# Two of the four sums of each block of w_out made by accumulating transfers in three of four column groups of a hybrid encoder layer

## The chip, the cores and the metric

The kernel runs on one core of a Trainium2 chip. The metric is the device time of one launch in microseconds, the median of several runs. The reader needs the names of the engines as the profile has them: PE multiplies matrices (PEld is its loading of weights), DVE and ACT work elementwise, POOL is a third elementwise engine that can also issue transfers, and SP issues nearly all transfers between HBM and the core's memory.

## The reference

One layer of an encoder on 512 tokens of width 2048, in float32. The input is normalised and multiplied by `w_in`. One part of the result goes through attention of 8 heads, another through a gated linear recurrence; both are normalised and gated. What matters here is the last step: the two halves are put side by side (512 x 2048) and multiplied by `w_out` (2048 x 2048), and the input is added:

```
mixed = jnp.concatenate([rms_norm(attn_out, attn_norm_w) * jax.nn.silu(g_attn),
                         rms_norm(lru_out, lru_norm_w) * jax.nn.silu(g_lru)], axis=-1)
return x + jnp.einsum('bse,ed->bsd', mixed, w_out)
```

## The kernel before

Every float32 product is made of three products of rounded parts: a matrix is cast to a high part on ACT (`wh`, `mh`), the rest is the low part, made by a subtraction on DVE (`wl`, `ml`), and PE multiplies high by high, high by low and low by high.

The last stage is `outputs` (L699 on). It works through `w_out` in four column groups of 512 columns (`c`), and in each group through eight blocks of 256 rows (`i`, 0 to 7 below). Six blocks (0 to 5) are multiplied by a scheme of Strassen's kind (Winograd's form): the block of 256 x 512 is cut into four quarters of 128 x 256, and seven products (`P1`, `Q6`, `Q5`, `Q7`, `P2`, `Q3`, `Q4`, L655) stand in place of eight. `mult` (L714) issues them, 42 matmuls of 256 columns for a block; `P1` needs only quarters of the block itself, `Q6` comes second and needs a sum. Blocks 6 and 7 are multiplied as they are (`whole`, L732). The left side has been split and summed beforehand.

What a block of the first kind needs before PE can take it, in `seven` (L674):

- `wraw` (L186) loads the block, 512 KB, from SP into a tile `wr`, of which there are three (L192).
- `combine` (L660) makes four sums of quarters into `t4`, a tile of 128 x 4 x 256 (the profile calls it `t`), of which there are two. The first two quarters, `src[:, 0]` and `src[:, 1]`, are the upper half of the block (its first 128 rows), left and right; the change calls them b12 and b11. `src[:, 2]` and `src[:, 3]` are the lower half, left and right. L665 makes the first two sums with one instruction, b11 + b12 and lower left + b12; L666 adds the lower left quarter to the first of them, and L667 adds the lower right one to the result.
- ACT casts three quarters of the block and then the four sums to the high parts (both L679), and DVE subtracts for the low parts (both L680). The tiles for these, `wkept` (L690), exist three times over: a block can be cast once PE is done with the block three before it.

For blocks 6 and 7 `four` (L682) casts and subtracts the quarters alone (L684, L685). After block 5 the products are put together on ACT (L775) and DVE (L776 to L779) and added to the input tile `xt` (L782); after block 7 DVE adds the remaining sums (L788, four adds for the four blocks of tokens) and SP stores each result (L789). The input for the next group is loaded by L708. In the first group, the left sides of the last blocks are still being made (`next(work)`, L758).

The order on PE is written out by hand. On the other engines a scheduler sets it: the blocks' preparation is given a high priority (`tc.high_priority(AHEAD)`), and each engine, SP and POOL among them, takes its instructions in the order in which the scheduler has put them; one that waits holds up those behind it. A tile that is used again can be written once its last reader is done.

Of the kernel before, what the change touches and what calls it, by code (L numbers as in the profile page):

```python
# [13 lines left out]
ALU = mybir.AluOpType  # L14
AX = mybir.AxisListType

P = 128
SEQ = 512
# [27 lines left out]
H = 256  # L46
# [9 lines left out]
def hybrid_kernel(  # L56
# [20 lines left out]
    nc = tc.nc  # L77
# [28 lines left out]
    def nm(s):  # L106
        cnt[0] += 1
        return f"{s}_{cnt[0]}"
# [30 lines left out]
    def f(ap):  # L139
        return ap.bitcast(F32)  # L140
# [45 lines left out]
    def wraw(w, r0, c0, nk=1):  # L186

        raw = pools["wr"].tile([P, 2, SEQ], F32, tag="wr", bufs=3, name=nm("wr"))
        src = w[r0 : r0 + 2 * P, c0 : c0 + SEQ].rearrange("(k p) e -> p k e", p=P)
        for k in range(nk):  # L190
            ks = slice(k * 2 // nk, (k + 1) * 2 // nk)
            nc.sync.dma_start(raw[:, ks, :], src[:, ks, :])  # L192
            yield raw
# [434 lines left out]
    def fin_s(shape=(P, SEQ)):  # L628
        return pools["fin"].tile(list(shape), F32, tag="s", bufs=2, name=nm("s"))
# [27 lines left out]
    def halves(t):  # L657
        return t.rearrange("p k (j e) -> p (k j) e", e=H)

    def combine(src, op):  # L660

        res = pools["fin"].tile([P, 4, H], F32, tag="t4", bufs=2, name=nm("t4"))
        a = nc.vector.tensor_tensor
        if op == ALU.add:
            a(res[:, 0:2], src[:, 1:3], src[:, 0:1].broadcast_to([P, 2, H]), op=op)  # L665
            a(res[:, 2], res[:, 0], src[:, 2], op=op)  # L666
            a(res[:, 3], res[:, 2], src[:, 3], op=op)  # L667
        else:
            a(res[:, 0:2], src[:, 0:1].broadcast_to([P, 2, H]), src[:, 1:3], op=op)
            a(res[:, 2], src[:, 1], res[:, 1], op=op)  # L670
            a(res[:, 3], src[:, 3], res[:, 2], op=op)
        return res

    def seven(src, op, hi, lo):  # L674

        src = halves(src)
        res = combine(src, op)
        for to, part in ((slice(0, 3), src[:, 1:4]), (slice(3, 7), res)):
            nc.scalar.copy(hi[:, to], part)  # L679
            nc.vector.tensor_sub(lo[:, to], part, f(hi[:, to]))  # L680

    def four(src, hi, lo):  # L682
        src = halves(src)
        nc.scalar.copy(hi, src)  # L684
        nc.vector.tensor_sub(lo, src, f(hi))  # L685
# [4 lines left out]
    def wkept(n):  # L690
        i = turn_of[0] % 3
        turn_of[0] += 1
        pool = pools["out" if i else "fin"]
        return [
            pool.tile([P, 7, H], F32R, tag=f"{t}{i}", bufs=1, name=nm(t))[:, :n]
            for t in ("wh", "wl")
        ]

    def outputs(work):  # L699

        for c in range(DM // SEQ):
# [12 lines left out]
            def mult(k, s, ah, al, a, bh, bl, b_, last):  # L714
                ts_ = slice(s * P, (s + 1) * P)
                if k in acc:
                    dst, bank = acc[k][:, s, :], k
                else:
                    bank = s if k == Q4 else 2 + s
                    dst = own[bank][:, H:] if k in (P2, Q4) else own[bank][:, :H]  # L720
                for lh, rh in ((ah, bh), (ah, bl), (al, bh)):
                    nc.tensor.matmul(  # L722
                        dst, lh[:, a, ts_], rh[:, b_, :], start=bank in fresh,
                        stop=last and s == 1 and rh is bh and lh is al, skip_group_check=True,
                    )
                    fresh.discard(bank)
# [5 lines left out]
            def whole(t, ah, al, bh, bl, last):  # L732

                ts_ = slice(t % 2 * P, (t % 2 + 1) * P)
                for half in range(2 if t == 1 and end else 1):
                    for k in range(2):
                        a, w = 2 * k + t // 2, slice(2 * k, 2 * k + 2)
                        dst = own[t].rearrange("p (j e) -> p j e", e=H)
                        if t == 1 and end:
                            dst, w = lasts[half], 2 * k + half  # L740
                        for j, (lh, rh) in enumerate(((ah, bh), (ah, bl), (al, bh))):
                            new = t == 1 and end and half == 0 and k == 0 and j == 0 and not last
                            nc.tensor.matmul(  # L743
                                dst, lh[:, a, ts_], rh[:, w], start=new,
                                stop=last and k == 1 and j == 2, skip_group_check=True,
                            )

            for i, (r0, A) in enumerate(mixed):
                with tc.high_priority(AHEAD):
                    (raw,) = wraw(w_out, r0, c * SEQ)  # L750
                    if i < 6:
                        bh, bl = wkept(7)
                        seven(raw, ALU.add, bh, bl)
                    else:
                        bh, bl = wkept(4)
                        four(raw, bh, bl)
                if c == 0:
                    next(work, None)  # L758
                    A = mixed[i][1]
                ah, al = A  # L760
                if i < 6:
                    for k in (P1, Q6, Q5, Q7, P2, Q3, Q4):
                        for s in range(2):
                            mult(k, s, ah, al, k[0], bh, bl, k[1], i == 5 and k in (P1, Q6, Q5, Q7))
                else:
                    for t in (2, 3, 0, 1):
                        whole(t, ah, al, bh, bl, i == 7)
                if i == 5:
                    with tc.high_priority(AHEAD):

                        def blk(i, j):
                            return comb[:, 2 * i : 2 * i + 2, j * H : (j + 1) * H]

                        v2 = fin_s((P, 2, H))
                        nc.scalar.copy(blk(1, 1), acc[P1])  # L775
                        nc.vector.tensor_sub(v2, acc[Q6], blk(1, 1))  # L776
                        nc.vector.tensor_add(blk(1, 0), acc[Q5], v2)
                        nc.vector.tensor_add(blk(0, 0), acc[Q7], blk(1, 0))
                        nc.vector.scalar_tensor_tensor(  # L779
                            blk(0, 1), acc[Q7], -1.0, v2, op0=ALU.mult, op1=ALU.subtract  # L780
                        )
                        nc.vector.tensor_add(xt, xt, comb)  # L782
# [124 lines left out]
    def build(i, pair, where, n=7):  # L907
        mixed[i][1] = hi, lo = where(n)
        if n == 7:
            seven(pair, ALU.subtract, hi, lo)  # L910
        else:
            four(pair, hi, lo)
# [28 lines left out]
    def last_gates():  # L941
# [11 lines left out]
        yield  # L953

    outputs(last_gates())
    closed("out", "wr", "cp")
    closed("fin", "hq")
# [41 lines left out]
```

## Time and profile before

| | |
|---|---|
| Median of three runs | 668.37 us (668.06 to 668.39) |
| The profiled execution's own time | 668.27 us |
| Its span in the profile | 666.5 us |
| DVE, ACT, POOL busy | 486.1, 331.1, 56.8 us |
| Bytes read from and written to HBM | 66.25 MB, 4.19 MB |
| PE's granted clock in the span | 1.00 |

The span runs from the first to the last instruction on the core; the execution's own time has the launch around it as well. A row of instructions by line gives the engine, the line, the operation, what it writes from what (`t<-wr`), how many there are, and the least, middle and longest duration of one in ns. A row of the timeline gives start and duration in us. A row of the transfers gives how many, their size, and the middle time from issue to landing in us. "SPq" is the queue of transfers that SP issues.

### The profile page before, as it was taken

What the parts mean: (1) busy time and instruction counts of PE and PEld (TensorE: products, weight loads), DVE (VectorE), ACT (ScalarE), POOL (GpSimd) and SP (SyncE); (2) the same over time, 40 slices, a digit from 0 to 9 for tenths busy, and PEclk for the clock granted to TensorE, in tenths of its full rate; (3) what the DMA queues carried; (4) which work ended last, traced back from release to release, by engine and by line L of the source; (5) the groups of instructions that cost most, each with busy time, mean ns of one, the idle gap of its engine ahead of it and who ended that gap; (6) DMA issues with size and microseconds to landing.
All of it is one profiled execution on the core that took longest, in us unless ns stands there. A gap on an engine that the chain in (4) does not pass through costs nothing.

```text
span 666.5 us, 9524 instructions
## 1 busy us (share of the span) xinstructions
PE 660.7 (99%) x3610; PEld 569.6 (85%) x3610; DVE 486.1 (73%) x819; ACT 331.1 (50%) x581; POOL 56.8 (9%) x77
## 2 busy tenths in 40 slices
PE   8999999999999999999999999999999999999997
PEld 6888888888888888888888888888889999899996
DVE  4879688978687754756955577449979994976944
ACT  4533898589766416345743455335436333332320
POOL 0000000000022203011222212110000000000000
PEclk9999999999999999999999999999999999999999
DMA  8842252323234412322112221232336364362711
GB/s 286 281 138 89 65 166 63 95 63 96 68 122 127 117 41 58 100 64 63 35 62 64 63 61 35 67 92 69 101 115 190 96 211 137 122 208 82 248 38 63
DMA packets 43773, 71.06 MB, mean 107 GB/s; under 512 B 2776, under 2 KB 13136, under 8 KB 43728
## 3 DMA queue, kind: packets, MB, share of 16 engines
q1 hardware_dynamic: 43696, 70.45, 34.5%
q8 instruction: 28, 0.46, 0.3%
q14 instruction: 17, 0.14, 0.1%
q10 hardware_dynamic: 32, 0.01, 0.0%
HBM read 66.25 MB, written 4.19 MB: 106 GB/s over the span
## 4 chain that ended last, share of the span: by engine, by line
PE 98%; DMA 1%; SPq 0%; DVE 0%; issue 0%
PE pj L143 20%; PE pj L145 20%; PE pj L144 20%; PE pj L722 10%; PE mm L722 8%; PE mm L743 6%; PE mm L145 3%; PE mm L143 3%; PE mm L144 3%; PE mm L568 2%; DMA b<-in_x_dram 1%; PE mm L229 1%; PE mm L516 1%; PE mm L266 0%; PE mm L636 0%; PE pj L743 0%
## 5 line engine op out<-in xcount | busy, mean ns | idle before, releaser
L143 PE MATMUL pj<-x,wh 128*128 128x512 f32 x384 | 153.1, 399 | 0.0
L145 PE MATMUL pj<-x,wl 128*128 128x512 f32 x384 | 149.9, 390 | 0.0
L144 PE MATMUL pj<-x,wh 128*128 128x512 f32 x384 | 149.7, 390 | 0.0
L203 ACT CAST wh<-wr 128x512 fp32r<-128x512 f32 x144 | 86.5, 617 | 81.2 <-PE pj L145 28.3
L204 DVE TENSOR_TENSOR wl<-wr,wh 128x512 fp32r<-128x512 f32 x144 | 100.6, 720 | 34.7 <-ACT wh L203 34.7
L145 PEld LDWEIGHTS pj<-x,wl 128*128 128x128 f32 x384 | 72.1, 188 | 15.4
L144 PEld LDWEIGHTS pj<-x,wh 128*128 128x128 f32 x384 | 72.3, 188 | 14.0 <-issue 0.5
L143 PEld LDWEIGHTS pj<-x,wh 128*128 128x128 f32 x384 | 72.2, 188 | 14.0 <-issue 0.5
L143 PE MATMUL pj<-wh,x 128*128 128x512 f32 x192 | 75.9, 395 | 0.0
L144 PE MATMUL pj<-wl,x 128*128 128x512 f32 x192 | 75.1, 391 | 0.0
L145 PE MATMUL pj<-wh,x 128*128 128x512 f32 x192 | 75.0, 391 | 0.0
L722 PE MATMUL pj<-wh,ml 128*128 128x256 f32 x192 | 54.1, 282 | 0.0
L722 PE MATMUL pj<-wh,mh 128*128 128x256 f32 x192 | 54.0, 281 | 0.0
L722 PE MATMUL pj<-wl,mh 128*128 128x256 f32 x192 | 53.8, 280 | 0.0
L679 ACT CAST wh<-wr 128x768 fp32r<-128x768 f32 x24 | 20.1, 836 | 60.9 <-issue 46.2
L570 ACT CAST b<-mm 128x512 fp32r<-128x512 f32 x32 | 18.8, 586 | 60.0 <-PE mm L568 60.0
L556 DVE TENSOR_REDUCE mx<-mm 128x1 f32<-128x512 f32 x32 | 22.1, 689 | 31.3 <-PE mm L145 30.8
L145 PEld LDWEIGHTS pj<-wh,x 128*128 128x128 f32 x192 | 36.1, 188 | 8.1
L143 PEld LDWEIGHTS pj<-wh,x 128*128 128x128 f32 x192 | 36.1, 188 | 8.0 <-issue 0.2
L144 PEld LDWEIGHTS pj<-wl,x 128*128 128x128 f32 x192 | 36.1, 188 | 7.9 <-issue 0.2
L722 PE MATMUL mm<-wh,ml 128*128 128x256 f32 x144 | 40.5, 282 | 0.0
L722 PE MATMUL mm<-wh,mh 128*128 128x256 f32 x144 | 40.5, 281 | 0.0
(203 smaller groups left out, 1322.3 us busy)
## 6 DMA issues: line engine op xcount, KB each, us to landing
wr<-in_w_in_dram SPq DMA_DIRECT2D x71, 512.0 KB, 3.6
wr<-in_w_out_dram SPq DMA_DIRECT2D x32, 512.0 KB, 3.8
xt<-in_x_dram SPq DMA_DIRECT2D x16, 256.0 KB, 4.4
out_dram<-xt SPq DMA_DIRECT2D x15, 256.0 KB, 3.6
b<-in_x_dram SPq DMA_DIRECT2D x7, 512.0 KB, 8.6
k<-in_lru_wa_dram SPq DMA_DIRECT2D x8, 128.0 KB, 3.7
k<-in_lru_wx_dram SPq DMA_DIRECT2D x8, 128.0 KB, 3.4
b<-in_x_dram SPq DMA_DIRECT2D x2, 256.0 KB, 4.9
```

The source lines that it names most:

```text
L143: nc.tensor.matmul(acc, lh, rh, start=start, stop=False)
L144: nc.tensor.matmul(acc, lh, rl, start=False, stop=False)
L145: nc.tensor.matmul(acc, ll, rh, start=False, stop=stop)
L203: nc.scalar.copy(hi, raw[:, k, :])
L204: nc.vector.tensor_sub(lo, raw[:, k, :], f(hi))
L229: nc.tensor.transpose(pt[:, t * P : (t + 1) * P], xc[:, t, ks], ident)
L556: nc.vector.tensor_reduce(mx, sc, axis=AX.X, op=ALU.max, negate=True)
L568: nc.tensor.transpose(pt[:, s * P : (s + 1) * P], p[:, s * P : (s + 1) * P], ident)
L570: nc.scalar.copy(pth[:, :, tt], p3)
L679: nc.scalar.copy(hi[:, to], part)
L722: nc.tensor.matmul(dst, lh[:, a, ts_], rh[:, b_, :], start=bank in fresh, stop=last and s == 1 and rh is bh and lh is al, skip_group_check ...
L743: nc.tensor.matmul(dst, lh[:, a, ts_], rh[:, w], start=new, stop=last and k == 1 and j == 2, skip_group_check=True,)
```

## The change

In `combine`, for the six blocks of the first kind in the column groups c = 1, 2 and 3 (`at` is None in the first group), the first instruction on DVE (L665) is replaced by three transfers. SP loads b11 into the first quarter of `t4` and the lower left quarter into the second, each 128 KB straight from `w_out` in HBM. POOL then issues one accumulating transfer, which adds b12 to both: it reads b12 from HBM twice (a source of step 0 over two) and adds it to what stands in `t4`. The first two quarters then hold the same two sums as before. The block itself is still loaded as before, and L666, L667 and all that follows stay as they are.

By the dependencies, the loads wait until `t4`'s buffer is free, the accumulating transfer waits for both loads, and L666 waits for the accumulating transfer.

```
-    def combine(src, op):
+    def combine(src, op, at=None):
 
         res = pools["fin"].tile([P, 4, H], F32, tag="t4", bufs=2, name=nm("t4"))
         a = nc.vector.tensor_tensor
         if op == ALU.add:
-            a(res[:, 0:2], src[:, 1:3], src[:, 0:1].broadcast_to([P, 2, H]), op=op)
+            if at:
+                r0, c0 = at
+                b12, b11 = (w_out[r0 : r0 + P, c0 + k * H : c0 + (k + 1) * H] for k in range(2))
+                nc.sync.dma_start(res[:, 0], b11)
+                nc.sync.dma_start(res[:, 1], w_out[r0 + P : r0 + 2 * P, c0 : c0 + H])
+                both = b12[:, None, :].broadcast_to([P, 2, H])
+                nc.gpsimd.dma_start(res[:, 0:2], both, accum_op=op)
+            else:
+                a(res[:, 0:2], src[:, 1:3], src[:, 0:1].broadcast_to([P, 2, H]), op=op)
             a(res[:, 2], res[:, 0], src[:, 2], op=op)
             a(res[:, 3], res[:, 2], src[:, 3], op=op)
...
-    def seven(src, op, hi, lo):
+    def seven(src, op, hi, lo, at=None):
 
         src = halves(src)
-        res = combine(src, op)
+        res = combine(src, op, at)
...
-                        seven(raw, ALU.add, bh, bl)
+                        seven(raw, ALU.add, bh, bl, (r0, c * SEQ) if c else None)
```

## Prediction

> **What bounds the kernel now.** I read the page's busy line first, then the waits of PE, then the chain of work that ended last.
>
> ```profile
> PE 660.7 (99%) x3610; PEld 569.6 (85%) x3610; DVE 486.1 (73%) x819; ACT 331.1 (50%) x581; POOL 56.8 (9%) x77
> PE mm L802 <- POOL ones L151: 1.1, 1, 1.1
> PE mm L229 <- DMA b<-in_x_dram: 0.9, 1, 0.9
> 540.15 2.80 PE pj L722 x24
> 581.12 2.80 PE pj L722 x24
> 621.72 2.88 PE pj L722 x24
> 646.64 2.88 PE pj L722 x24
> ```
>
> The second and third rows are all that PE waits for in the whole span: 2.0 us, both at the start. The output stage has no wait of PE at all. The last rows are pieces of the chain: the last three column groups begin on PE at 540.15, 581.12 and 621.72, so a group takes 41.0 and then 40.6 us, and the sixth block of the last group begins at 646.64. DVE, which the change relieves, is never what PE waits for. **So there is nothing to win on the path; the question is whether the longer preparation of a block still fits into 41 us a group.**
>
> **What is removed.** In 18 of the 24 blocks (six in each of three groups) the first sum of DVE goes; the other work on t, which I need below, stays.
>
> ```profile
> L665 DVE TENSOR_TENSOR t<-wr x24: 682/692/699, 485.1 to 630.1; 128x512 f32<-128x512 f32 x24
> L666 DVE TENSOR_TENSOR t<-t,wr x24: 414/424/430, 486.9 to 630.8; 128x256 f32<-128x256 f32 x24
> L667 DVE TENSOR_TENSOR t<-t,wr x24: 415/424/427, 487.3 to 631.3; 128x256 f32<-128x256 f32 x24
> L679 ACT CAST wh<-t x24: 1037/1047/1057, 487.8 to 637.5; 128x1024 fp32r<-128x1024 f32 x24
> L680 DVE TENSOR_TENSOR wl<-wr,wh x24: 948/954/964, 486.0 to 637.6; 128x768 fp32r<-128x768 f32 x24
> L680 DVE TENSOR_TENSOR wl<-t,wh x24: 1214/1224/1227, 489.0 to 638.5; 128x1024 fp32r<-128x1024 f32 x24
> ```
>
> 18 x 0.692 = 12.5 us leave DVE (first row). None of it lies on PE's chain, so the gain is 0; what hides it is PE's own work.
>
> **What is added.** For each of the 18 blocks: two loads of 128 KB into t on SP, a wait of POOL for both, one accumulating transfer of 256 KB (one quarter of w_out's block read twice and added to t), and a wait of DVE's L666 for it. POOL is idle there, as in this slice of the stage, so its 18 issues hold up no other work:
>
> ```profile
> 540.00:560.00 20.00, 20.00 (x171) 20.00 (x170) 14.31 (x21) 7.25 (x8) 0.00 (x0) 1.00 0.66 221
> ```
>
> (Columns: the slice, its length, then busy time of PE, PEld, DVE, ACT and POOL, granted clock, share and rate of the transfers.) SP's 36 issues are 36 x 0.37 = 13.3 us spread over 120 us, no price by themselves either. The price is in the order. Before, the sums took 0.69 + 0.42 + 0.42 us from the block's landing, and a buffer of t was held for little more. Now it is held from the issue of its first load on; there are two, and SP, POOL and DVE each take their instructions in order.
>
> ```profile
> wr<-in_w_out_dram SPq DMA_DIRECT2D x32, 512.0 KB, 3.8
> xt<-in_x_dram SPq DMA_DIRECT2D x16, 256.0 KB, 4.4
> b<-in_x_dram SPq DMA_DIRECT2D x7, 512.0 KB, 8.6
> k<-in_lru_wx_dram SPq DMA_DIRECT2D x8, 128.0 KB, 3.4
> b<-in_x_dram SPq DMA_DIRECT2D x2, 256.0 KB, 4.9
> out_dram<-xt SPq DMA_DIRECT2D x2, 128.0 KB, 2.3
> L192 SPq DMA_DIRECT2D wr<-in_w_out_dram x32: 367/368/432, 481.2 to 633.6; - x32
> L789 SPq DMA_DIRECT2D out_dram<-xt x17: 332/356/360, 538.1 to 663.3; - x17
> ```
>
> The last number of the first six rows is the time from issue to landing; the last two rows are SP's time per issue. A load of 128 KB is 3.4 (the fourth row), the pair 0.37 + 3.4 = **3.8 us**.
>
> The accumulating transfer, called **A** from POOL's issue to its landing, is shown nowhere: no row has POOL issue one or a transfer add. Bounds by the nearest rows: 2.3 us (the fastest, a store of 128 KB) and 8.6 us (512 KB of x, twice the bytes, which is what an add that reads its target as well would move). Its own size is nearest to the 256 KB loads, 4.4 and 4.9. I take the upper of them, rounded: **A = 5.0**, since it has a target to read too.
>
> **The chain that sets a group's length.** I follow the order in which the changed program's instructions stand on each engine, from one point to the same point a group later: the end of the second L680 of a group's first block (block 0). The rows that it needs beside those above:
>
> ```profile
> 609.73 0.68 DVE L776 TENSOR_TENSOR s<-pj,cb 128x512 f32<-128x512 f32 x1
> 610.66 0.69 DVE L777 TENSOR_TENSOR cb<-pj,s 128x512 f32<-128x512 f32 x1
> 611.59 0.68 DVE L778 TENSOR_TENSOR cb<-pj,cb 128x512 f32<-128x512 f32 x1
> 612.19 0.68 DVE L779 SCALAR_TENSOR_TENSOR cb<-pj,s 128x512 f32<-128x512 f32 x1
> 612.91 2.29 DVE L782 TENSOR_TENSOR xt<-xt,cb 128x2048 f32<-128x2048 f32 x1
> 534.45 1.23 DVE L680 TENSOR_TENSOR wl<-t,wh 128x1024 fp32r<-128x1024 f32 x1
> 623.17 0.69 DVE L788 TENSOR_TENSOR xt<-mm,xt 128x512 f32<-128x512 f32 x1
> L685 DVE TENSOR_TENSOR wl<-wr,wh x8: 1217/1220/1227, 520.6 to 647.8; 128x1024 fp32r<-128x1024 f32 x8
> 591.00 0.84 ACT L679 CAST wh<-wr 128x768 fp32r<-128x768 f32 x1 [3.12 <-issue]
> 591.87 0.96 DVE L680 TENSOR_TENSOR wl<-wr,wh 128x768 fp32r<-128x768 f32 x1 [1.08 <-ACT wh L679]
> ```
>
> (a) Block 2's t takes block 0's buffer, so its two loads start there: 3.8, then its sum, A. (b) On DVE, L666 of block 2 stands ahead of the last L788 of the group before; that add releases the last output store, and on SP the second load of block 3's t stands behind that store: 0.42 + 0.69 + 0.36 + 3.4 = 4.9, then the sum of block 3, A. (c) L666, L667, the cast of t and its L680: 0.42 + 0.42 + 1.05 + 1.22 = 3.1; that frees the buffer for block 5. (d) Block 5's loads 3.8, its sum A. From here two ways lead on.
>
> (e) By the sums: L666, L667, cast, L680 of block 5, 3.1; its buffer goes to block 1 of the next group: loads 3.8, sum A, then L666, L667 and block 7's L685, 0.84 + 1.22 = 2.1. (e') By the blocks themselves: L666, L667 and the first L680 of block 5, 1.8, free a buffer of wr; the next group's block 0 is loaded, 3.8; L666, L667, L685 of block 6, 2.1; block 1 is loaded, 3.8; L666, L667, L685 of block 7, 2.1.
>
> (f) Both go on with L776 to L782, 0.68 + 0.69 + 0.68 + 0.68 + 2.29 = 5.0, which stand ahead of block 0's two L680, 0.95 + 1.22 = 2.2, where the round closes.
>
> Handing over from engine to engine costs hundredths (the cast from 591.00 ends at 591.84, DVE starts at 591.87); I put 0.5 us a round. So by (e): 3.8 + 4.9 + 3.1 + 3.8 + 3.1 + 3.8 + 2.1 + 5.0 + 2.2 + 0.5 = 32.3 plus 4 A; by (e'): 3.8 + 4.9 + 3.1 + 3.8 + 1.8 + 3.8 + 2.1 + 3.8 + 2.1 + 5.0 + 2.2 + 0.5 = 36.9 plus 3 A. At A = 5.0 that is 52.3 and 51.9: **a round of 52.3 us where PE needs 41**. DVE's load doesn't make it, the waits in series do.
>
> **The sum.** In the first of the three groups block 0's second L680 ends at 534.45 + 1.23 = 535.7; its own t and that of block 1 are loaded ahead, so I leave that point. Two rounds of 52.3 take it to 640.3 in the last group. There (a) to (d) and block 5's 3.1 follow: 3.8 + 4.9 + 3.1 + 3.8 + 3.1 + 0.3 = 19.0 plus 3 A = 34.0, to 674.3. PE needs that L680 with the seventh matmul of block 5, in the profile at 646.64 + 6/24 x 2.88 = 647.4; from there to the end of the span, 666.5, are 19.1 us. New span: 674.3 + 19.1 = 693.4. The profiled execution took 668.27 us around a span of 666.5, 1.8 more: **695 us**, against 668.27 (0.1 under the median of the three runs, 668.37): +4.0%. Each us on A is worth 2 x 4 + 3 = 11 us, each us off it about 9.
>
> **Rivals.**
>
> *Not slower.* The mechanism is the same round with a sum so short that PE's lead covers it. For no change the two rounds and the rest must end at 668.3 - 1.8 - 19.1 = 647.4, that is 111.7 us after 535.7: 2 x 36.9 + 19.0 + 9 A = 111.7 gives A = 2.1. Below that, or if the lead of two blocks that a group starts with takes up more than I count, the time is 668, and PE without waits leaves no more to win than that. Against it: 2.1 is below every landing row above, the smallest being a store of half the size. Chance 6%, 1 of them for a small gain.
>
> *A short sum*, hardly longer than the smallest transfer: A = 2.3 gives 535.7 + 2 x 43.8 + 25.9 + 19.1 + 1.8 = 670. The Trainium skill, page "DMA: Bandwidth & Descriptors", section "Anatomy of one DMA — SWDGE (gpsimd) path", gives a transfer issued by GpSimd about 2.0 us plus its bytes over 436 GB/s, an estimate of 2.6 us for 256 KB, by which the sum would be 673; no row here shows such a transfer, and the loads of this size from SP at 4.4 speak against so little. Chance of A between 2.1 and 3: 12%.
>
> *A long sum.* POOL's issue, the reading of the target and the adding may come one after the other. A = 8.6 gives rounds of 32.3 + 34.4 = 66.7 and a last part of 44.8: 535.7 + 133.4 + 44.8 + 19.1 + 1.8 = 735. For it: nothing in the profile says that the add is free. Chance of A above 6.5: 18%.
>
> *Crowding.* A block's traffic grows from 512 KB to 1024 KB and more with the target read. If the 128 KB loads take 4.4 in place of 3.4, by the row of the 256 KB loads, (e) has four of them: 4 x 1.0 x 2 + 3 x 1.0 = 11 us more, 706. Against it: blocks of 512 KB land in 3.8 while SP has little else. Chance 10%.
>
> **How the numbers follow.** The forecast, A from 3 to 6.5, holds 54%, crowding 10, a long sum 18, a short one 12, not slower 6. The range takes the bounds of A, 670 at 2.3 and 735 at 8.6, and leaves out "not slower" and about half of the long sums, some 15 in 100. What a measurement of this kernel can tell from no change is about 0.2%, 1.3 us: faster 1%, within 3% (most of "not slower" is a last stall of under 1.3 us, the rest a little more), slower 96%.
>
> **What would show it.** In the changed profile PE waits at L722 in the last three groups, on L680 of DVE, a few times a group and some 25 us in all; these groups begin about 52 us apart. L666 waits on the accumulating transfer, whose landing after POOL's issue is A; the second load of block 3 goes out right behind the fourth output store. DVE's busy time falls by 12.5 us while it idles more. I am wrong in the size if the sum lands in another time than 5.0, and wrong in the mechanism if PE waits in the first blocks of a group without L666 having waited, or if the groups grow while the sums land in under 3 us.

## The result, and the profile after

| | before | after |
|---|---|---|
| Median | 668.21 us (668.06 to 668.39, four runs) | 726.62 us (725.69 to 728.11, four runs) |
| Profiled execution and its span | 668.27, 666.5 us | 726.36, 724.5 us |

The ratio is 1.0876, with a 95% interval from 1.0863 to 1.0888: 8.8% slower. The forecast was 695, 4.0% slower. The time lies inside the range, but the loss is more than twice the one forecast.

The new lines in `combine` move the later ones down by 11: L665 is now L676, L666 and L667 are L677 and L678, L679 and L680 are L690 and L691, L685 is L696, L722 and L743 (PE) are L733 and L754, L776 to L779 are L787 to L790, L782 is L793, L788 and L789 are L799 and L800. The two new loads are L671 and L672, the accumulating transfer is L674. In some kernels of the experiments the lines are one less or up to four more.

The page of after, its busy line, the row of the queue for POOL's transfers (packets, MB, share) and the rows of the transfers around `w_out` (the last number is the middle time from issue to landing):

```profile
PE 680.3 (94%) x3610; PEld 583.1 (80%) x3610; DVE 475.4 (66%) x801; ACT 330.7 (46%) x581; POOL 78.4 (11%) x95
q0 software_dynamic: 4896, 4.72, 4.3%
wr<-in_w_out_dram SPq DMA_DIRECT2D x32, 512.0 KB, 4.4
t<-in_w_out_dram SPq DMA_DIRECT2D x36, 128.0 KB, 4.2
t<-in_w_out_dram POOLq DMA_DIRECT2D x18, 256.0 KB, 6.0
```

A, the time from POOL's issue to the landing of its sum, is 6.0 in the middle, not 5.0. The new loads take 4.2 where 3.4 was assumed, and the block's own load went from 3.8 to 4.4. DVE lost 10.7 us of work (486.1 to 475.4) and the kernel lost 58. L674 itself, from the rows of that line:

```profile
L674 POOL DMA_DIRECT2D t<-in_w_out_dram x18: 1199/1205/1383, 518.4 to 695.4; - x18
DMA to landing us min/median/max: 4.1/6.0/8.8
```

What PE waits for in the last stage of after, which had no wait before (total, number of times, longest):

```profile
PE mm L733 <- DVE xt L799: 18.8, 5, 7.1
PE pj L733 <- DVE wl L691: 12.7, 16, 2.7
PE mm L754 <- DVE wl L696: 5.2, 3, 2.8
PE pj L733 <- ACT wh L690: 1.5, 2, 1.1
```

These are 18.8 + 12.7 + 5.2 + 1.5 = 38.2 us. PE's busy time also rose, from 660.7 to 680.3, with the same 3610 matmuls: 19.6 us. Together 57.8, the growth of the span (58.0). One reason why the same matmuls take longer is seen behind the longest wait. The slices of after around it (columns as in the prediction: slice, length, PE, PEld, DVE, ACT, POOL, granted clock, share and rate of the transfers):

```profile
603.00:604.00 1.00, 1.00 (x10) 0.93 (x8) 0.00 (x0) 0.00 (x0) 0.00 (x0) 1.00 0.79 245
605.00:611.00 6.00, 0.00 (x0) 0.00 (x0) 0.85 (x2) 0.00 (x0) 1.03 (x1) 0.84 0.65 170
612.00:613.00 1.00, 1.00 (x7) 1.00 (x6) 0.75 (x2) 1.00 (x2) 0.00 (x0) 0.50 0.87 314
614.00:615.00 1.00, 1.00 (x6) 1.00 (x6) 0.72 (x1) 0.00 (x0) 0.12 (x1) 0.50 0.83 219
615.00:616.00 1.00, 1.00 (x7) 1.00 (x6) 0.00 (x0) 0.00 (x0) 1.00 (x1) 0.54 1.02 267
616.00:617.00 1.00, 1.00 (x11) 1.00 (x10) 0.00 (x0) 0.00 (x0) 0.09 (x1) 1.00 1.10 335
```

PE stands for 7.1 us up to 611.2, then its clock is granted at half, and a microsecond holds 6 or 7 matmuls in place of 11; from 616 on it runs at full speed again. The stage has seven stretches at the half clock, 34.1 us in all with PE busy for 28.4 of them (the granted clock over the span is 0.976). At half speed that is some 14 of the 19.6 us, an estimate; where the other 5 lie is open. The Trainium skill, page "TensorE: Matmul & The Clock Gate", section "Part 1: The HAM clock gate (the "warmup" mystery)", says that the clock is halved after an idle window of about 3.4 us and restored after about as long of steady work. The trace agrees in kind, with longer times: the mean of 0.84 from 605 to 611 puts the fall to half at about 609, some 5 us after the last matmul, and the matmuls then run about 4.5 us at half speed.

**The round, term by term.** The forecast followed a round from the end of block 0's second L691 to the same point of the next group. The timeline of DVE in after has the four points, three starts of a group and block 5 of the last one:

```profile
535.98 1.22 DVE L691 TENSOR_TENSOR wl<-t,wh 128x1024 fp32r<-128x1024 f32 x1
597.98 1.22 DVE L691 TENSOR_TENSOR wl<-t,wh 128x1024 fp32r<-128x1024 f32 x1
663.17 1.22 DVE L691 TENSOR_TENSOR wl<-t,wh 128x1024 fp32r<-128x1024 f32 x1
703.62 1.23 DVE L691 TENSOR_TENSOR wl<-t,wh 128x1024 fp32r<-128x1024 f32 x1 [0.25 <-ACT wh L690]
```

The ends are 537.2, 599.2, 664.4 and 704.85: rounds of 62.0 and 65.2 us where 52.3 were forecast, and a last part of 40.5 where 34.0 were. From 704.85 to the end of the span are 19.65 (forecast 19.1). The second round in the chain of work that ended last (start, duration, what; rows between them left out):

```profile
599.62 4.53 DMA t<-in_w_out_dram
604.22 0.61 issue
604.83 5.24 DMA t<-in_w_out_dram
610.15 0.43 DVE t L677
610.58 0.07 DVE xt L799
611.20 2.58 DMA out_dram<-xt
614.88 8.77 DMA t<-in_w_out_dram
623.67 0.43 DVE t L677
625.67 1.24 DVE wl L691
627.30 5.77 DMA t<-in_w_out_dram
633.20 0.61 issue
633.81 5.83 DMA t<-in_w_out_dram
639.66 0.43 DVE t L677
```

The steps (a) to (d) stand there in the forecast's order: loads of block 2, its sum, L677 with L799 behind it, block 3's sum, L677 to L691, loads and sum of block 5. They stand so in the last part, too. The chain names the output store at 611.20 for the way into block 3's sum; SP's own timeline shows what lies between, the second load of block 3 behind the last three stores:

```profile
601.83 0.33 SPq L671 DMA_DIRECT2D t<-in_w_out_dram  x1
602.43 9.11 SPq L800 DMA_DIRECT2D out_dram<-xt  x3
611.59 0.43 SPq L672 DMA_DIRECT2D t<-in_w_out_dram  x1
```

| Step | forecast, us | after, us |
|---|---|---|
| (a) two loads of block 2 | 3.8 | 4.9 (599.23 to 604.17) |
| its sum | 5.0 | 5.2, and 0.7 before POOL starts it |
| (b) L677, L799, store, second load of block 3 | 4.9 | 4.7 (610.15 to 614.88), POOL's start in it |
| its sum | 5.0 | 8.8 |
| (c) L677 to L691 | 3.1 | 3.2 |
| (d) two loads of block 5 | 3.8 | 6.2 (626.92 to 633.09) |
| its sum | 5.0 | 5.8, and 0.7 before it |
| (e) L677 to L691 of block 5 | 3.1 | 3.2 |
| loads of the next block 1 | 3.8 | 5.0 (642.90 to 647.93), POOL's start in it |
| its sum | 5.0 | 7.3 (647.93 to 655.23) |
| L677, L678, L696, then (f) | 9.3 | 9.1 (655.25 to 664.39) |

From 639.66 to 647.93 the printed chain goes by the next block 0's own load (641.44, 5.14), as in (e'), and its L677 and L678, up to 647.60. By the dependencies, POOL's sum there needs the two loads of block 1; the second, issued at 643.28, lands 4.0 us later, 0.7 before POOL starts, as at the other sums. The two ways end within half a microsecond of each other, and the table follows (e).

The sums are 27.1 together in place of 20.0, 7.1 of the 12.9 us by which this round is over the forecast. POOL starts each of these four some 0.6 to 0.7 us after its loads have landed (the "issue" at 604.22 and 633.20), 2.6 in all; the loads make about the remaining 3. What DVE and ACT do between the transfers came out as forecast.

The first round, of 62.0 us, leaves the forecast's steps behind block 3's sum. The chain goes on by the sum of block 4, the next block 0 and PE's matmuls of block 6 (585.35, 5.52). POOL's timeline has the sums of blocks 3 and 4:

```profile
553.80 1.21 POOL L674 DMA_DIRECT2D t<-in_w_out_dram  x1 [10.55 <-DMA t<-in_w_out_dram]
561.15 1.20 POOL L674 DMA_DIRECT2D t<-in_w_out_dram  x1 [6.15 <-issue]
```

The chain has POOL's wait for block 4's loads end at 555.12, yet its transfer starts only at 561.15, just behind the landing of block 3's sum (553.80 + 7.03). It is the same with block 4 in the other two groups, at 623.97 and 687.21: POOL's next sum starts 0.32 us after the one before has landed. The forecast let the sums of two blocks run beside each other. What this costs by itself is not shown, for block 5's way (e) runs beside it: its second L691 ends at 577.75, and the sum of the next block 1 starts 6.0 us later, where the second round took 5.0.

### The profile page after: what moved, and what is told of

It reads as the page before. It is cut to its first block, busy times and chain, and to the rows that moved or that the text cites. A ratio compares the mean times of both kernels' runs of the same rounds, so it can differ in the third digit from the quotient of the medians.

```text
span 724.5 us, 9697 instructions
## 1 busy us (share of the span) xinstructions
PE 680.3 (94%) x3610; PEld 583.1 (80%) x3610; DVE 475.4 (66%) x801; ACT 330.7 (46%) x581; POOL 78.4 (11%) x95
## 3 DMA queue, kind: packets, MB, share of 16 engines
q0 software_dynamic: 4896, 4.72, 4.3%
## 4 chain that ended last, share of the span: by engine, by line
PE 72%; DMA 14%; DVE 7%; issue 4%; ACT 1%; SPq 0%; DVEq 0%; POOLq 0%
PE pj L143 18%; PE pj L145 18%; PE pj L144 18%; DMA t<-in_w_out_dram 13%; PE mm L145 3%; PE mm L143 3%; PE mm L144 3%; DVE wl L691 3%; PE mm L754 2%; PE mm L568 2%; ACT wh L690 1%; PE mm L229 1%; DVE t L677 1%; PE pj L733 1%; DMA wr<-in_w_out_dram 1%
## 5 line engine op out<-in xcount | busy, mean ns | idle before, releaser
L690 ACT CAST wh<-t 128x1024 fp32r<-128x1024 f32 x24 | 25.0, 1047 | 106.0 <-DVE t L678 106.0
L733 PE MATMUL pj<-wl,mh 128*128 128x256 f32 x192 | 60.2, 314 | 12.7 <-DVE wl L691 12.7
L677 DVE TENSOR_TENSOR t<-t,wr 128x256 f32<-128x256 f32 x24 | 10.1, 423 | 94.0 <-DMA t<-in_w_out_dram 78.9
L733 PE MATMUL pj<-wh,mh 128*128 128x256 f32 x192 | 58.6, 305 | 1.5 <-ACT wh L690 1.5
L733 PE MATMUL mm<-wh,mh 128*128 128x256 f32 x144 | 41.9, 291 | 18.8 <-DVE xt L799 18.8
L733 PE MATMUL pj<-wh,ml 128*128 128x256 f32 x192 | 58.5, 305 | 0.0
L733 PEld LDWEIGHTS pj<-wl,mh 128*128 128x128 f32 x192 | 41.0, 213 | 16.4 <-DVE wl L691 16.3
L674 POOL DMA_DIRECT2D t<-in_w_out_dram x18 | 21.9, 1216 | 227.9 <-DVE t L678 91.5
L570 ACT CAST b<-mm 128x512 fp32r<-128x512 f32 x32 | 18.8, 586 | 60.0 <-PE mm L568 60.0
L733 PEld LDWEIGHTS mm<-wh,mh 128*128 128x128 f32 x144 | 28.2, 196 | 19.8 <-DVE xt L799 19.8
L733 PEld LDWEIGHTS pj<-wh,mh 128*128 128x128 f32 x192 | 41.0, 214 | 2.0 <-ACT wh L690 1.9
```

What stands on the lines that cost most here:

```text
L570: nc.scalar.copy(pth[:, :, tt], p3)
L674: nc.gpsimd.dma_start(res[:, 0:2], both, accum_op=op)
L733: nc.tensor.matmul(dst, lh[:, a, ts_], rh[:, b_, :], start=bank in fresh, stop=last and s == 1 and rh is bh and lh is al, skip_group_check ...
```

## The experiments

Each kernel ran once with a profile; the kernel before measured 668.1 to 668.6 beside them. The theory is the forecast's: the time is the waits in series (loads, POOL, sum, DVE) through two buffers. The rivals are that the added bytes crowd the other transfers, that one wait (the one for L799, the buffer, the stores) is the whole loss, or that the adding makes the transfer slow. The four runs of after lie 2.4 us apart, so less than that between two kernels that wait as it does says nothing.

**The transfer without the add.**

```
-                nc.gpsimd.dma_start(res[:, 0:2], both, accum_op=op)
+                nc.gpsimd.dma_start(res[:, 0:2], both)
```

> The change as it is, but POOL's transfer copies the quarter b12 into both places of t and doesn't add; the sums of b11 and of the lower left quarter are left out, all waits and the number of transfers stay. Theory of waits in series (the added time is latency of four sums a group, one after the other, whatever the transfer does): the transfer lands 5.5 to 6 us after POOL's issue as in the changed kernel (6.0), time 715 to 727. Rival, the add is dear: the transfer lands like a load of 256 KB in the profile of before, 4.4 to 4.9, so about 11 landings x 1.3 us = 14 us less, 712 or under. A landing near 4.4 with an unchanged time would speak against both.

707.69 us. From its page, the rows of the queue and the transfers, and from the rows of L674:

```profile
q0 software_dynamic: 1440, 4.72, 2.9%
t<-in_w_out_dram SPq DMA_DIRECT2D x36, 128.0 KB, 3.1
t<-in_w_out_dram POOLq DMA_DIRECT2D x18, 256.0 KB, 5.1
```

```profile
L674 POOL DMA_DIRECT2D t<-in_w_out_dram x18: 722/724/894, 519.0 to 679.3; - x18
```

This kernel leaves two sums out. The same bytes as a plain copy land in 5.1 rather than 6.0, POOL's issue takes 0.72 rather than 1.2 us, and the loads beside it take 3.1 rather than 4.2. Also, the copy of block 4 starts at 553.58 while that of block 3 (551.67, landing 6.5 us later) is still in flight. All this together is worth 19 of the 58 us. The other 39 stay without any add: they are the price of the waits in series. The time is on the side of the rival (712 or under), the landing on neither's (5.1); neither theory had it whole.

**The same loads, the sum on DVE.**

```
-                nc.gpsimd.dma_start(res[:, 0:2], both, accum_op=op)
+                a(res[:, 0:2], res[:, 0:2], src[:, 0:1].broadcast_to([P, 2, H]), op=op)
```

> The two loads into t stay, but DVE adds b12 in place (0.69 us, the same sums); no transfer on POOL. Waits in series: a step of loading and summing falls from some 11.7 us (5.7 from the loads' issue to POOL's start, 6.0 to the landing) to about 5.2, four steps a round save 26 us, so a round of 62 to 65 falls under PE's 41 and the time is 668 to 675. Rival, crowding by bytes: the loads are half of the bytes that the change adds, so about half of the 58 us stays, 690 to 700.

669.98 us. PE's waits in its last stage are one row:

```profile
PE mm L732 <- DVE xt L798: 1.1, 1, 1.1
```

The 36 extra loads, their place on SP and the buffer's longer hold, all kept, cost 1.7 us. So steps (a), (b) and (d) alone break nothing; POOL's transfer in the middle does. Without it a round by the forecast's own (e) needs 32.3 us and four sums on DVE of 0.69, 35.1 in all against PE's 41, and the wait goes.

**No loads, the accumulating transfer kept.**

```
-                nc.sync.dma_start(res[:, 0], b11)
-                nc.sync.dma_start(res[:, 1], w_out[r0 + P : r0 + 2 * P, c0 : c0 + H])
+                nc.scalar.copy(res[:, 0:2], src[:, 1:3])
```

> The accumulating transfer stays, but the two loads into t are replaced by one copy on ACT from the block that is there already (0.6 us), the same sums. Waits in series: a step is the block's landing, the copy and 6.6 us for the sum in place of 5.7 + 6.0; four steps save 4 x 5 = 20 us a round, but the copy now waits for the block, whose load stands in SP's order: 695 to 710, PE waiting less than half as long as in the changed kernel. Crowding by bytes: also about half of 58 us, so the time alone tells little here; the landing of the blocks does (4.4 in the changed kernel, 3.8 before).

699.57 us: 27 less than the change, still 31 more than before. A is 5.1 (4.1 to 8.1). The sum behind its block and a copy of ACT costs 31 without the loads, the loads cost 1.7 without the sum, and the two in series 58: the loads count only with POOL's transfer behind them.

**The same transfers with nobody waiting.** Before's kernel, with the three transfers of a block issued from POOL into tiles that nothing reads:

```
+                    if c and i < 6:
+                        o = pools["out"].tile([P, 2, H], F32, tag="o", bufs=3, name=nm("o"))
+                        nc.gpsimd.dma_start(o[:, 0], w_out[r0 : r0 + P, c * SEQ + H : (c + 1) * SEQ])
+                        nc.gpsimd.dma_start(o[:, 1], w_out[r0 + P : r0 + 2 * P, c * SEQ : c * SEQ + H])
+                        o2 = w_out[r0 : r0 + P, c * SEQ : c * SEQ + H][:, None, :].broadcast_to([P, 2, H])
+                        nc.gpsimd.dma_start(o, o2, accum_op=ALU.add)
```

> The kernel before, and beside it the change's three transfers per block, with the same bytes, all issued by POOL into spare tiles that nobody reads. Waits in series: PE doesn't wait in the output stage, 667 to 671. Crowding by bytes: blocks land late and PE waits, 690 or more.

669.21 us, and no wait of PE in the last stage. Its page:

```profile
wr<-in_w_out_dram SPq DMA_DIRECT2D x32, 512.0 KB, 4.7
o<-in_w_out_dram POOLq DMA_DIRECT2D x18, 256.0 KB, 5.7
```

The traffic is there and the blocks land later (4.7 for 3.8), but it costs 1 us. Crowding is no cause by itself; it lengthens transfers, and by this run that counts only where something waits for them one after the other.

**A third buffer of t.** Every third block's tile comes from another pool:

```
-        res = pools["fin"].tile([P, 4, H], F32, tag="t4", bufs=2, name=nm("t4"))
+        third = at and (at[0] // (2 * P) + 4) % 8 % 3 == 2
+        pool, n = ("out", 1) if third else ("fin", 2)
+        res = pools[pool].tile([P, 4, H], F32, tag="t4", bufs=n, name=nm("t4"))
```

> The change, with a third buffer for t (one more tile, used by every third block), so that a block's loads into t needn't wait for the L691 of the block two before. Waits in series through the two buffers: the chain of four sums a round is cut, sums of neighbouring blocks run beside each other, 690 to 707. Rival, the order of the queues sets the time whatever the buffers: 718 to 728.

709.62 us, 17 less than the change and a little above what was expected. A is 5.8. PE's wait for L691 falls from 12.7 to 6.0, the one for L799 is 20.0. The expectation had the sums of neighbouring blocks beside each other, and they still follow one another: the one issued at 555.39 lands 8.0 us later, and the next starts at 563.72.

**The output stores issued by ACT**, so that the second load of block 3 is not behind them on SP:

```
-                    nc.sync.dma_start(
+                    nc.scalar.dma_start(
                         of[rows_[t], cs.start + e0 : cs.start + e1], xt[:, t, e0:e1]
```

> The change, with the output stores issued by ACT in place of SP, so that the second load of block 3's t goes out right behind the first. If that load behind the stores is one of the four steps in series, as the prediction had it, block 3's sum starts up to 10 us earlier in each group until another step is last: 700 to 716, and the second load's issue follows the first by 0.4 us. Rival, the stores' place is harmless, since block 3 would have waited anyway: 723 to 728.

711.70 us, 15 less. On SP the two loads now follow each other, from its timeline:

```profile
596.11 0.33 SPq L671 DMA_DIRECT2D t<-in_w_out_dram  x1
596.49 0.84 SPq L672 DMA_DIRECT2D t<-in_w_out_dram  x1
```

Step (b) is real, and there are three places where a group hands over to a changed one: about 5 us each. A is also lower here, 5.4, and how much of the 15 us comes by that is not shown.

**Both together.** The edits of the last two kernels in one.

> The third buffer for t and the stores on ACT together; each alone took 17 and 15 us off 726.6. If they cut two different steps of the chain, the savings add: 690 to 698. If both cut the same wait, no more than the larger: 705 to 712. Left over in either case is the chain of one buffer's loads, sum, cast and subtraction, so it stays over 680.

700.64 us, 26 less than the change: between 32, the sum of the two savings, and one of them alone. They free parts of the same chain. With both gone the kernel is still 32 us slower than before, and A (4.9 here), the loads (4.8), POOL's start and the sums one behind the other remain.

**The last group only.**

```
-                        seven(raw, ALU.add, bh, bl, (r0, c * SEQ) if c else None)
+                        seven(raw, ALU.add, bh, bl, (r0, c * SEQ) if c == 3 else None)
```

> The change in the last column group alone. Waits in series: the round from one group to the next is what costs (62 and 65 us in the changed kernel, against 41), and the last group has only the part from its block 0 to its block 5, 40.5 us as measured there: 617.2 + 40.5 + 19.7 + 1.8 = 679, give or take 4. Rival, each group that has the transfers costs the same, a third of 58 us: 688.

686.24 us, 7 above the first theory's number and within 2 of the rival's 688. Block 0's second L691 of the last group ends at 619.93 + 1.22 = 621.15, and block 5's at 663.3 (the rows of the timeline start at 619.93 and 662.08): a last part of 42.2, like the 40.5 of after. The start, too, is 4 us later than the 617.2 that the unchanged groups before would give, so the sums of blocks 0 and 1 are not made ahead for nothing. One changed group costs 18 us, three cost 58: the last group alone costs about as much as each of the three.

**Half the bytes.** One load and one accumulating transfer of 128 KB; DVE makes the other sum:

```
-                nc.sync.dma_start(res[:, 1], w_out[r0 + P : r0 + 2 * P, c0 : c0 + H])
-                both = b12[:, None, :].broadcast_to([P, 2, H])
-                nc.gpsimd.dma_start(res[:, 0:2], both, accum_op=op)
+                nc.gpsimd.dma_start(res[:, 0], b12, accum_op=op)
+                a(res[:, 1], src[:, 2], src[:, 0], op=op)
```

> The change for one of the two sums: one load of 128 KB, one accumulating transfer of 128 KB; DVE makes the second sum (0.42 us). The results are those of the change. If the accumulating transfer's time is mostly fixed (issue, latency), it lands in 4.8 to 5.5 us (6.0 with 256 KB) and the time is 702 to 715; if it goes by its bytes, it lands in 3.2 to 3.9 and the time is 682 to 698.

690.34 us. Its page:

```profile
q0 software_dynamic: 2592, 2.36, 2.3%
t<-in_w_out_dram POOLq DMA_DIRECT2D x18, 128.0 KB, 3.3
```

**The same bytes in rows of 2 KB.** One row of two quarters per partition as the source; the second sum is then b11 plus the lower left quarter:

```
-                both = b12[:, None, :].broadcast_to([P, 2, H])
-                nc.gpsimd.dma_start(res[:, 0:2], both, accum_op=op)
+                both = w_out[r0 : r0 + P, c0 : c0 + 2 * H]
+                nc.gpsimd.dma_start(res[:, 0:2].rearrange("p k e -> p (k e)"), both, accum_op=op)
```

> The change, but the accumulating transfer adds one row of 2 KB per partition (b12 and b11 side by side) in place of b12 twice in rows of 1 KB, so that the second sum is b11 + lower left quarter, not the one that is wanted; bytes and order stay. In the changed kernel an accumulating transfer leaves 4896/18 = 272 packets, the plain one of the same size 1440/18 = 80, the half one 2592/18 = 144. If the time goes by pieces, the transfer now has about 144 and lands in 4 to 4.8 us, time 700 to 714. If it goes by bytes, it lands in 5.5 to 6.2 as before, time 720 to 730.

715.63 us. Its page:

```profile
q0 software_dynamic: 2592, 4.72, 4.1%
t<-in_w_out_dram SPq DMA_DIRECT2D x36, 128.0 KB, 3.3
t<-in_w_out_dram POOLq DMA_DIRECT2D x18, 256.0 KB, 5.9
```

The two kernels issue 18 transfers of 2592 / 18 = 144 packets each, with POOL's issue at 0.855 us in both, and differ in bytes: 3.3 against 5.9. So A goes by its bytes rather than by its packets (the first kernel also has one load less beside each; the least landings, 3.0 and 3.9, are less far apart). The packets have a price elsewhere: with 144 in place of 272 the loads nearby take 3.3 rather than 4.2, and the time is 11 us less. One more thing has changed. The sums of blocks 3 and 4 in the kernel with rows of 2 KB:

```profile
553.14 0.87 POOL L674 DMA_DIRECT2D t<-in_w_out_dram  x1 [10.78 <-DMA t<-in_w_out_dram]
555.07 0.86 POOL L674 DMA_DIRECT2D t<-in_w_out_dram  x1 [1.06 <-DMA t<-in_w_out_dram]
```

The first lands 8.0 us after its issue, and the second starts long before that. So it is not the program's order that keeps the sums of after apart; in these kernels it goes with the form of the transfer, 272 packets against 144. Whether the 11 us come from the shorter loads or from sums beside each other is not separated.

**The source in the core's memory.** The accumulating transfer adds the quarter from the block that has been loaded, not from HBM:

```
-                both = b12[:, None, :].broadcast_to([P, 2, H])
+                both = src[:, 0:1].broadcast_to([P, 2, H])
```

> The change, with b12 read from the block in the core's memory and not from HBM; the sum now also waits for the block. If reading HBM twice is what makes the sum long, it lands in under 4.8 us; if it is the pieces and the adding, it lands in 5.4 to 6.2. The time, 700 to 730, depends on the added wait for the block as well and decides nothing.

707.05 us, A 4.5 (3.8 to 9.9). The middle is 1.5 us under that of after, the least only 0.3 (3.8 against 4.1). The sum now waits for the block, too, and the same transfer from HBM has its middle anywhere from 4.9 to 6.0 in the other kernels. So reading HBM is at most a part of A; how large is not settled, and the larger part stays.

**L799 ahead of L677.** The last add of the group before is put ahead of the first L677 of block 2 in DVE's order:

```
-            a(res[:, 2], res[:, 0], src[:, 2], op=op)
+            after = tc.issue_after(added[-1].ins) if at and (at[0] // (2 * P) + 4) % 8 == 2 else ExitStack()
+            with after:
+                a(res[:, 2], res[:, 0], src[:, 2], op=op)
...
+    added = []
...
-                    nc.vector.tensor_add(xt[:, t, e0:e1], src, xt[:, t, e0:e1])
+                    added.append(nc.vector.tensor_add(xt[:, t, e0:e1], src, xt[:, t, e0:e1]))
```

> The change, with one pair of instructions in another order on DVE: the last add of a group's output (L799) stands ahead of the add that waits for block 2's accumulating transfer (L677), not behind it. In the changed kernel PE waits 18.8 us for that L799, the most of all, and SP's last store and block 3's second load wait for it too. If that place is one step of the chain (the one that the stores on ACT also took out, 15 us), the time is 706 to 714, PE no longer waits for L799, and its waits move to L691. If PE's wait for L799 costs by itself beside that step, both go: 690 to 704. If neither, 722 to 728.

712.00 us. PE's waits:

```profile
PE pj L737 <- DVE wl L693: 17.2, 14, 3.1
PE mm L758 <- DVE wl L698: 6.7, 4, 2.4
PE mm L737 <- DVE xt L803: 0.6, 1, 0.6
```

The largest wait of after, 18.8 for that add, is all but gone, and the time falls only by 15, as when the stores left SP: the add releases the stores, and these the second load of block 3. Here, too, A is lower, 5.1. The rest of PE's idle time has moved to the wait for the blocks' own parts.

None of these kernels beats the one before. The two without a wait for POOL's transfer come within 1.0 and 1.7 us of it.

## Why the prediction was right in direction and wrong in size

**"There is nothing to win on the path": right.** DVE lost 10.7 us and no part of it showed.

**"Waits in series, not DVE's load": right, and shown.** The loads without the sum cost 1.7 us, all the transfers without a reader cost 1.0, the sum without the loads 31, the whole 58. The steps (a) to (d) stand in the chain of after in the order forecast in the second round and the last part; from there way (e) sets the second round by the landings, with (e') half a microsecond beside it. The first round goes another way behind block 3's sum.

**"A = 5.0" failed: it is 6.0**, and up to 8.8 in the second round. By the forecast's own rule, 11 us on the time for each us of A, that is 11 of the missing 32 (726.6 less 695). The reason that it gave for the upper of the two 256 KB loads, the target to be read, was too weak a step: the copy of the same bytes from POOL already lands in 5.1, and the add comes on top. Nor is A one number: the same transfer lands in 5.1 with L799 ahead and in 4.9 with the third buffer and the stores on ACT, so the 6.0 is that of this order of the transfers. The sum of block 3 takes 7.0, 8.8 and 7.2 us in the three groups, each time beside the four loads of xt (L719); that these lengthen it was not tried. The Trainium skill, page "DMA: Bandwidth & Descriptors", section "Anatomy of one DMA — SWDGE (gpsimd) path", gives about 2.0 us plus the bytes over 436 GB/s, an estimate of 2.6 us for such a transfer; the runs do not bear it out, neither for the add (least 4.1) nor for the copy (middle 5.1, least 3.5).

**"A load of 128 KB is 3.4" failed: 4.2 beside these transfers.** The page of before had 3.7 for another row of this size. Crowding was put down as a rival with 10%, to hold in place of the forecast, at 706. It holds together with the longer A: 11 pairs of loads at 0.8 more are 9 us. That it is the adding's packets rather than the bytes is what the copy (3.1) and the rows of 2 KB (3.3) speak for.

**"0.5 us a round for handing over" failed for POOL.** The row that it came from was between ACT and DVE. From the landing of the loads to POOL's start it is 0.6 to 0.7 where nothing else holds POOL, by the forecast's steps four times a round and three in the last part: 11 x 0.6 = 6.6 us. The three terms give 695 + 11 + 9 + 7 = 722, or 720 without the 1.3 that the forecast had already put for handing over, of 726.6. Of the rest, 1.5 are the later starting point (537.2 for 535.7) and 0.6 the end (19.65 for 19.1). The last 3 to 4 are not settled term by term; single sums of 7 and 8.8 us, the blocks' own loads at 4.4 and the first round's other way are where they would lie.

**The overlap of two sums was put at nothing and failed.** The forecast has block 4's sum beside the steps of blocks 3 and 5 at no price. In after POOL starts no sum before the one before has landed, which kept block 4's waiting in all three groups, by 6.0 us in the first (555.12 to 561.15).

**The wait for L799 was not foreseen.** The prediction used L799's place behind L677 for the stores alone. The same add also frees what PE writes next, and there PE stood longest, up to 7.1 us at a time. Its cost is not shown to be a term of its own: with L799 moved ahead, 18.8 us of PE's wait went and 14.6 of time, about what the stores on ACT gave, while waits at L693 and L698 grew.

**The forecast of PE's idle time, some 25 us, was 38.2**, with 19.6 more of busy time in the same matmuls, some 14 of it by the half clock. From the start of the second round to the end of the last part PE's matmuls do not appear in the chain, so there the half clock lengthens work that has slack; what it costs elsewhere was not tried.

**The signs named beforehand.** DVE's 18 instructions are gone, with 10.7 us of busy time rather than 12.5. L677 waits on the accumulating transfer, and L733 on L691 in the three groups: seen. Block 3's second load right behind the fourth store: seen, at 611.59. Groups 52 us apart: 62 and 65.

## What to carry to other kernels

To move work from an engine with slack to a transfer is to trade a duration of tenths (here 0.69 us) for one of microseconds, with the issue and the hand-over ahead of it (here 4.2, 0.6 and 6.0); count it by the buffers through which the steps follow each other, not by any engine's busy time. A transfer costs little while nothing waits for it: the same bytes cost 1 us unread and 58 in a chain through two buffers. Where several terms of such a chain are estimates, add their upper ends together, for here the same traffic came with longer loads and a longer sum at once.

## What the runs showed of the hardware that was not expected

An accumulating transfer of 256 rows of 1 KB makes 4896 / 18 = 272 packets, the plain copy of the same rows 1440 / 18 = 80, and one of 128 rows, whether of 1 or 2 KB, 144: which fits one packet a row and 16 more, where the copy would have one for four rows and 16 more. POOL's issue goes with it: 1.2 us for 256 rows with the add, 0.855 for 128, 0.72 for the copy. The landing goes by the bytes instead (3.3 us for 128 KB, 5.9 for 256 KB at the same number of packets; least 3.0 and 3.9), and with the added values read from the core's memory in place of HBM the middle landing is 1.5 us less, the least 0.3. Two accumulating transfers of 272 packets are never in flight together in after, nor in the kernels with the third buffer, the stores on ACT or L799 ahead: the next starts 0.3 us or more after the landing of the one before. Those of 144 packets and the copies of 80 do overlap. Why is not shown.
